# Feature-major chunks in the Mamba-2 layer of a fused attention and state-space kernel

## The chip, the cores and the metric

The kernel runs on one core of one Trainium2 chip. The time is that of one launch on the device, in microseconds, as the median of several runs. Beside it stands one profiled execution, with its trace: start and duration of every instruction on TensorE (PE, with its weight loads PEld), VectorE (DVE), ScalarE (ACT), GpSimd (POOL) and the queue of SyncE (SP), which issues most DMAs.

## The reference

Two layers over 1024 latent tokens and 256 context tokens, width 1024: windowed attention, then a gated bidirectional Mamba-2 (SSD) mixer, which is where the change lies. Cut to that layer:

```
z, xbc, dt_raw = split(h @ w_in)                       # h: adaLN-modulated, normalized
xbc = silu(centred_depthwise_conv(xbc, conv_w, conv_b)) # 5 taps
xs, bm, cm = split(xbc)                                # 8 groups x 4 heads x 64; state 128
dt = softplus(dt_raw + dt_bias)                        # per direction and head
# per direction, in chunks of 128 tokens (a_cs: cumulative sum of dt * A in the chunk)
states = einsum(bm, exp(a_last - a_cs), xs * dt)       # carried from chunk to chunk: h_prev
y_diag = einsum(cm . bm, exp(a_cs_q - a_cs_s), xs * dt)
y_off  = einsum(cm, h_prev, exp(a_cs))
y = y_diag + y_off                                     # of both directions
u = (y_f + y_b + d_skip * xs) * silu(z)
u = u * rsqrt(mean(u * u over a group's 256) + 1e-6)   # per token and group
y_lat = (u * norm_w) @ w_out
h = h + gate * y_lat;  out = rms_normalize(h) * final_norm_w
```

## The kernel before, in words

Activations lie feature-major: 128 features on the partitions, tokens along the free dimension. Big products run in the type fp32r, each as three matmuls: operands are split into a high and a low part (`uH`, `uL` of the layer's input; `wh`, `wl` of a weight tile), and high times high, low times high and high times low are added in PSUM. Smaller products (chunks, states, transposes) run in plain fp32, where one product is two records in the trace (a transpose is one).

The SSD layer (`ssd`) loops over 8 groups, and in each over 8 chunks of 128 latent tokens; group and chunk make a *slot* (`slot`, 64 of them, numbered n). While the slots of group g run, the input projection of group g + 1 (`front`, a generator) is cut into pieces, which `fill(0)` to `fill(4)` deal out inside the slot in the shares of `SEGS`; while the last group's slots run, the output projection (`ssd_out`) takes that place. So PE always has projection matmuls between the slot's small products. The pieces are in model units (`N512`, `N256`, `FRONT`, `OUT`), which only divide the work. Their side work (splitting weights, the convolution's taps, silu) waits in the queue `post` and is taken out at a steady pace. Beside the slots runs the generator `states`, which prepares the next group's context and backward states, a step at each `tick`. The framework then orders the instructions of each engine and of SP's queue by a plan of its own, before the run; on the chip each engine executes its list in that order and waits where an input is late. A wait holds up all that stands behind it on the same engine.

`front` (group g): four x, B and C tiles of 128 features over context and latent tokens (L1143, L1152), then convolution and silu; B and x are also transposed to token-major (`bn`, `xn`). The gate z comes last (L1177): here the token block of `uH`/`uL` is the stationary operand, 128 tokens by 128 of the contraction, and 256 columns of the weight move, so z comes out token-major; tanh and one DVE operation make `sz`.

`slot`, in the order of the code:

- `pcb` = B . C of the chunk (L1282); `po`, the inter-chunk product of C with the forward and the backward state, 256 columns each (L1284, L1285), token-major.
- `M`, the decays of both directions for four heads (`decays`: a predicated copy on DVE, four exponentials on ACT), times `pcb` on DVE (L1286). The rows of cumulative sums for it are loaded by SP two slots ahead (`load_rows`, tiles `fd`, `bd`); POOL adds an offset to `bd` (`offset`).
- the state's step: decay on POOL, product `S` (L1291), addition on DVE.
- `y2` = `po` times exp(a_cs), which lies token-major in `eacs` (L1295).
- `dg`, the diagonal of `pcb`, and `sk`, the skip factor with what the two directions share on the diagonal; POOL multiplies x by `sk`, adds the two halves of `y2`, and adds the former (L1306 to L1308).
- `yd` = M . x, four products of 64 columns (L1311, M stationary); DVE adds it and multiplies by `sz`; ACT squares with a sum, POOL takes the power -0.5, ACT rescales (L1320 to L1329).
- in the next slot, `tail`: two transposes back to feature-major (L1341), each evacuated by ACT with the norm weight (L1342), and a store to DRAM (`uN_d`).

PSUM for these is a ring of three buffers (`psX`): `pcb`, `po`, `S`, `yd` and the tail's tile take them in turn.

`ssd_out` loads the 32 half-rows of features (`feats`, 128 x 512 each), splits them into high and low parts (ACT, DVE) and multiplies by the weights in sweeps (L1571); the last tokens' rows are used at the end of the last sweep.

## Time and profile before

| | us |
|---|---|
| median of 3 runs | 1819.04 (1817.78 to 1820.63) |
| the profiled execution, its own time | 1818.37 |
| its span, first to last instruction | 1816.6 |
| PE busy / DVE / ACT / POOL | 1749.0 / 1166.0 / 869.9 / 811.1 |

The span is what the trace shows; the execution's own time is 1.8 us longer. The attention layer and the norms fill the first 750 us or so, the SSD layer the rest: the first group's projection up to 857 us, the slots from there to 1700, the rest of the output projection and the final norm after that. In the lines of the profile, "x512" is a count, "| busy, mean ns" follow it, and "<-" names what ended the idle time before. In the timeline the first two numbers are start and duration.

### The profile page before, as it was taken

The page shows a single profiled execution, that of the slowest core. Times are in us where ns is not written, and L with a number is a line of the kernel's source. Part 1 is how long each engine was busy: PE and PEld are TensorE (multiplying, and loading weights), DVE is VectorE, ACT ScalarE, POOL GpSimd, SP SyncE. Part 2 cuts the span into 40 slices and gives each one's busy share as a digit, 9 for nine tenths or more (in the row PEclk, how much of TensorE's full clock was granted, in tenths as well). Part 3 has the DMA queues.
Part 4 walks back from the last instruction along what each step waited for, and adds up shares of the span by engine and source line. Part 5 has one row for each costly group of instructions (what it writes and reads, how often), then busy time and mean ns, then how long its engine had stood idle before and what let it go on. Part 6 is the DMA issues. An engine that isn't in the chain of part 4 may idle for free.

```text
span 1816.6 us, 29129 instructions
## 1 busy us (share of the span) xinstructions
PE 1749.0 (96%) x10379; PEld 1500.2 (83%) x10379; DVE 1166.0 (64%) x2125; ACT 869.9 (48%) x1895; POOL 811.1 (45%) x1074
## 2 busy tenths in 40 slices
PE   6999998999999899999999999999999999999997
PEld 3797767788889687778898898989889898988886
DVE  3563536786787766675766748567675857766643
ACT  3521235677788766352444434344353434544522
POOL 2441127554456465303454544646454454644311
PEclk9999999999999999999999999999999999999998
DMA  8768865543345445311322323323332322655542
GB/s 296 285 156 255 261 192 138 119 116 99 99 117 132 118 133 195 112 42 52 86 68 79 93 69 88 82 71 79 78 93 78 82 79 74 188 163 179 163 137 70
DMA packets 209393, 227.89 MB, mean 125 GB/s; under 512 B 16096, under 2 KB 149088, under 8 KB 208224
## 3 DMA queue, kind: packets, MB, share of 16 engines
q1 hardware_dynamic: 175184, 207.38, 38.1%
q0 software_dynamic: 34064, 18.65, 5.6%
q8 instruction: 82, 1.34, 0.3%
q14 instruction: 63, 0.52, 0.1%
HBM read 191.14 MB, written 35.13 MB: 125 GB/s over the span
## 4 chain that ended last, share of the span: by engine, by line
PE 83%; DVE 5%; ACT 4%; DMA 4%; issue 3%; POOL 0%; SPq 0%; DVEq 0%; ACTq 0%; POOLq 0%
PE pj L1152 17%; PE pj L1177 10%; PE pj L1571 7%; PE pj L223 6%; PE pj L225 6%; PE pj L224 6%; PE psD L1143 3%; PE pt L694 3%; PE psX L1311 2%; PE pv L701 2%; PE psD L1236 2%; PE pv L700 2%; PE S L669 2%; PE psX L1285 1%; PE S L670 1%
## 5 line engine op out<-in xcount | busy, mean ns | idle before, releaser
L223 PE MATMUL pj<-uH,wh 128*128 128x256 f32 (+1 forms) x652 | 233.5, 358 | 8.1 <-DVE rope_b L532 2.3
L224 PE MATMUL pj<-uL,wh 128*128 128x256 f32 (+1 forms) x652 | 220.1, 338 | 0.0
L225 PE MATMUL pj<-uH,wl 128*128 128x256 f32 (+1 forms) x652 | 220.1, 338 | 0.0
L211 POOL TENSOR_TENSOR wl<-wr,wh 128x512 fp32r<-128x512 f32 x92 | 121.7, 1326 | 97.4 <-ACT wh L209 96.9
L1152 PE MATMUL pj<-uH,wh 128*128 128x512 f32 x480 | 161.4, 410 | 2.0 <-ACT xn L1088 1.2
L1152 PE MATMUL pj<-uH,wl 128*128 128x512 f32 x480 | 158.5, 403 | 0.0
L1152 PE MATMUL pj<-uL,wh 128*128 128x512 f32 x480 | 157.3, 402 | 0.0
L699 DVE TENSOR_TENSOR pl<-pt,ph 128x512 fp32r<-128x512 f32 x168 | 114.2, 687 | 61.3 <-ACT ph L698 60.4
L223 PEld LDWEIGHTS pj<-uH,wh 128*128 128x128 f32 x652 | 124.7, 191 | 34.9 <-issue 8.6
L1177 PE MATMUL pj<-wh,uH 128*128 128x256 f32 x512 | 148.0, 289 | 3.1 <-ACT xn L1088 3.0
L1177 PE MATMUL pj<-wl,uH 128*128 128x256 f32 x512 | 150.7, 294 | 0.0
L1213 POOL TENSOR_TENSOR xw<-xn,dtdec 128x256 f32<-128x256 f32 x144 | 92.9, 649 | 127.1 <-PE psD L1236 108.5
L1177 PE MATMUL pj<-wh,uL 128*128 128x256 f32 x512 | 149.5, 292 | 0.0
L1342 ACT ACTIVATE uT<-psX,nw 128x128 f32<-128x128 f32 x128 | 46.7, 365 | 193.2 <-PE psX L1341 193.1
L225 PEld LDWEIGHTS pj<-uH,wl 128*128 128x128 f32 x652 | 124.4, 191 | 14.8 <-issue 1.7
L673 DVE CUSTOM_DVE_ANT_0 sm<-S,mask,nsink 128x640 f32<-128x640 f32 (+2 forms) x160 | 118.7, 772 | 26.5 <-PE S L670 14.5
L224 PEld LDWEIGHTS pj<-uL,wh 128*128 128x128 f32 x652 | 124.9, 192 | 11.5 <-issue 2.8
L209 ACT CAST wh<-wr 128x512 fp32r<-128x512 f32 (+1 forms) x132 | 84.8, 645 | 102.5 <-PE pj L224 78.7
L698 ACT CAST ph<-pt 128x512 fp32r<-128x512 f32 x168 | 97.5, 585 | 64.5 <-PE pt L694 58.9
L675 ACT ACTIVATE sm<-sm,nm 128x640 f32<-128x640 f32 (+2 forms) x160 | 118.5, 742 | 12.6 <-DVE nm L673 12.3
L1152 PEld LDWEIGHTS pj<-uL,wh 128*128 128x128 f32 x480 | 90.1, 188 | 19.0
L1152 PEld LDWEIGHTS pj<-uH,wh 128*128 128x128 f32 x480 | 89.1, 188 | 19.6 <-ACT bn L1088 2.0
(383 smaller groups left out, 4999.8 us busy)
## 6 DMA issues: line engine op xcount, KB each, us to landing
fd<-acs SPq DMA_DIRECT2D x64, 256.0 KB, 5.0
bd<-acs SPq DMA_DIRECT2D x64, 256.0 KB, 5.2
wr<-w_x SPq DMA_DIRECT2D x31, 512.0 KB, 3.8
wr<-w_sk SPq DMA_DIRECT2D x24, 512.0 KB, 4.0
wr<-wg SPq DMA_DIRECT2D x44, 256.0 KB, 4.6
qs<-q POOLq DMA_DIRECT2D x40, 256.0 KB, 3.9
wr<-wo SPq DMA_DIRECT2D x40, 256.0 KB, 2.7
wada<-w_ad SPq DMA_DIRECT2D x8, 1024.0 KB, 6.4
```

Of the source, the lines that this page charges most:

```text
L211: (eng or nc.vector).tensor_tensor(l, raw, h, op=ALU.subtract)
L223: self.nc.tensor.matmul(ps, lh, rh, start=first and i == 0, stop=False)
L224: self.nc.tensor.matmul(ps, lh, rl, start=False, stop=False)
L225: self.nc.tensor.matmul(ps, ll, rh, start=False, stop=last and i == n - 1)
L673: nc.vector.tensor_tensor_reduce(out=sm[:, :W], in0=Sv, in1=self.mask[:, m0 : m0 + W], scale=-SCALE, scalar=self.nsink[:, 4 * j + r : 4 * ...
L675: nc.scalar.activation(sm[:, :W], sm[:, :W], AF.Exp, bias=nm[:, r : r + 1], scale=-1.0, accum_out=sums[:, r : r + 1])
L698: nc.scalar.copy(ph, ptf)
L699: nc.vector.tensor_sub(pl, ptf, ph)
L1152: nc.tensor.matmul(raw[:, 512 * i : 512 * i + 512], l[:, k, :], r[i][:, k, :], start=k + y == 0, stop=k == KT - 1 and y == 2)
L1177: nc.tensor.matmul(pj[:, c], l, r[:, k, :], start=c % 2 + q + k + y == 0, stop=c % 2 == 1 and q == 1 and k == 3 and y == 2)
L1213: nc.gpsimd.tensor_tensor(xw, X(st, c).rearrange("p (r h) -> p r h", r=R), self.dtdec[:, c, hd(d, g)].unsqueeze(2).broadcast_to([P, R, HP] ...
L1571: nc.tensor.matmul(banks[x], l[:, z, sl], r, start=k == 2 * qs[0] and y == 0, stop=k == 2 * qs[-1] + 1 and y == 2)
```

## The change

The slot is turned from token-major to feature-major.

- `z` is computed like x: the weight tile is stationary, 512 tokens move; `w_z` is laid out in tiles of 128 features.
- `po` has the states as the stationary operand and C as the moving one: four products of 128 columns. Its factor exp(a_cs) now lies along the free dimension, the same on all partitions of a head: it is stored to DRAM once (`eacs_d`, 16 stores) and loaded by two broadcasting DMAs a slot (`load_scale`, tile `eb`), two slots ahead.
- The skip goes on M's diagonal: DVE makes `dg` and `sk` before `y2`; POOL multiplies the identity by `sk` (into the tile of `eb`, once `y2` has read it) and adds it to M. The product of x with `sk` and its addition to y are gone.
- `yd` has x as the stationary operand, 64 columns a head, and M moves, 128 columns; odd heads write the upper half of the partitions, even heads the lower half.
- y is stored without its norm. ACT squares it, POOL adds the two halves (`sq`), and the tail is one product of `sq` with a column of ones, one small ACT operation, and in every fourth slot a power on POOL over four columns and a store of 512 factors (`rn_d`).
- `ssd_out` loads those factors with a broadcast (`scales`, in the buffers of `bT` and `cT`), POOL multiplies each feature tile by them, ACT applies the norm weight while it makes the high part, DVE makes the low part with the weight in the same operation.
- `SEGS` gives the first stretch of a slot 3.5 of 9.8 shares (1.5 of 9.9 before). At start-up four transposes and four copies go, since `eacs` is not made token-major any more.

The core of the diff, dedented; `ps2` gets three buffers for `yt` and two for `eb`:

```diff
 N512, N256 = 0.229, 0.120
-FRONT = 4 * 48 * N512 + 3 * 24 * N256 + 8 * 24 * N256
+FRONT = 4 * 48 * N512 + 3 * 24 * N256 + 4 * 24 * N512
...
 LATE = 3.0
-SEGS = (1.5, 2.0, 2.0, 2.2, 2.2)
+SEGS = (3.5, 1.8, 1.5, 1.5, 1.5)
...
 self.acs_d = t(dr, [1, 64, LAT], F32, "acs")
+self.eacs_d = t(dr, [2, G, 2, 2, LAT], F32, "eacsd")
...
 nc.scalar.activation(acs, acs, AF.Exp)
+for d in range(2):
+    for f in range(2):
+        for r in range(R):
+            row = 64 * d + 32 * f + r
+            nc.sync.dma_start(self.eacs_d[r % 2, :, d, r // 2, 512 * f : 512 * f + 512], acs[row : row + 29 : 4, :512])
...
         pt = t(ps, [P, 4, 2, 2, 32], F32, "psX")
-        for x, y in enumerate((dd, acs, dt, ln)[: 1 if b == 4 else 4]):
+        for x, y in enumerate((dd, dt, ln)[: 1 if b == 4 else 3]):
...
             nc.scalar.copy(self.dtdec[:, c, :].rearrange("p f (d h) -> p d f h", d=2), pt[:, 0])
-            nc.scalar.copy(self.eacs[:, c, :].rearrange("p f (d h) -> p d f h", d=2), pt[:, 1])
-            nc.scalar.copy(self.dtb[:, c, :], pt[:, 2, 1])
-            nc.scalar.copy(self.vf[:, c, :], pt[:, 3, 0])
-            nc.vector.tensor_sub(self.vo[:, c, :], pt[:, 3, 1], self.vf[:, c, :])
+            nc.scalar.copy(self.dtb[:, c, :], pt[:, 1, 1])
+            nc.scalar.copy(self.vf[:, c, :], pt[:, 2, 0])
+            nc.vector.tensor_sub(self.vo[:, c, :], pt[:, 2, 1], self.vf[:, c, :])
...
 def wz(q):
-    return lambda: weights(a["w_z"][g, q], 4, 256)
+    return lambda: weights(a["w_z"][2 * g + q], KT, P)
...
 for i in range(2):
-    pj = t(ps, [P, 4, 256], F32, "pj2")
+    pj = t(ps, [P, 2, 512], F32, "pj2")
...
         need(ww)
-        for c in range(4):
-            for k in range(4):
-                u, v = uH[i][:, 4 * q + k, c * P : (c + 1) * P], uL[i][:, 4 * q + k, c * P : (c + 1) * P]
-                for y, (l, r) in enumerate(((u, ww["h"]), (u, ww["l"]), (v, ww["h"]))):
-
-                    nc.tensor.matmul(pj[:, c], l, r[:, k, :], start=c % 2 + q + k + y == 0, stop=c % 2 == 1 and q == 1 and k == 3 and y == 2)
-                    yield N256
+        for k in range(KT):
+            for y, (l, u) in enumerate(((ww["h"], uH), (ww["h"], uL), (ww["l"], uH))):
+                nc.tensor.matmul(pj[:, q], l[:, k, :], u[i][:, k, :], start=k + y == 0, stop=k == KT - 1 and y == 2)
+                yield N512
...
             post.extend(st["next"]["steps"])
-    sz = t(self.pz, [P, 4, 256], F32, "sz")
+    sz = t(self.pz, [P, 2, 512], F32, "sz")
...
         nc.vector.scalar_tensor_tensor(sz, in0=sz, scalar=1.0, in1=pj, op0=ALU.add, op1=ALU.mult)
-        st["sz"] += [sz[:, x] for x in range(4)]
+        st["sz"] += [sz[:, :, x * P : (x + 1) * P] for x in range(4)]
...
 self.uN_d = [t(self.dr, [2, P, P * NCH], F32, f"uN{g}") for g in range(G)]
+self.rn_d = [[t(self.dr, [1, 512], F32, f"rn{g}_{i}") for i in range(2)] for g in range(G)]
...
+eb = {}
+
+def load_scale(n):
+    if n < G * NCH:
+        g, c = divmod(n, NCH)
+        x = eb[n] = t(ps2, [P, 2, 2, P], F32, "eb")
+        for f in range(2):
+            src = self.eacs_d[f : f + 1, g, :, :, c * P : (c + 1) * P].rearrange("o d e q -> o (d e) q")
+            nc.sync.dma_start(x[64 * f : 64 * f + 64].rearrange("p d e q -> p (d e) q"), src.broadcast_to([64, R, P]))
+
...
 cs = slice(c * P, (c + 1) * P)
-xc = X(st, c).rearrange("p (r h) -> p r h", r=R)
...
 nc.tensor.matmul(pcb, st["bT"][:, cs], st["cT"][:, cs], start=True, stop=True)
-po = t(ps, [P, 512], F32, "psX")
-nc.tensor.matmul(po[:, :256], st["cT"][:, cs], flat(st["hf"]), start=True, stop=True)
-nc.tensor.matmul(po[:, 256:], st["cT"][:, cs], flat(st["hb"][c]), start=True, stop=True)
+po = t(ps, [P, 2, 2, P], F32, "psX")
+for d, h in enumerate((st["hf"], st["hb"][c])):
+    for e in range(2):
+        nc.tensor.matmul(po[:, d, e], flat(h)[:, e * P : (e + 1) * P], st["cT"][:, cs], start=True, stop=True)
...
     st["hf"] = hn
-y2 = t(ps2, [P, 2, R, HP], F32, "y2")
-nc.vector.tensor_tensor(y2, po.rearrange("p (d r h) -> p d r h", d=2, r=R),
-                        self.eacs[:, c, :].rearrange("p (d q) -> p d q", d=2)[:, :, 4 * g : 4 * g + 4].unsqueeze(3).broadcast_to([P, 2, R, HP]), op=ALU.mult)
+x = eb.pop(n)
+y2 = t(ps2, [P, 2, 2, P], F32, "y2")
+sk = t(ps2, [P, R + 1], F32, "sk")
+dg, sk = sk[:, R:], sk[:, :R]
+nc.vector.tensor_tensor_reduce(out=y2[:, 0, 0], in0=pcb, in1=self.ident, scale=1.0, scalar=0.0, op0=ALU.mult, op1=ALU.add, accum_out=dg)
+nc.vector.scalar_tensor_tensor(sk, in0=self.dtb[:, c, 4 * g : 4 * g + 4], scalar=dg, in1=self.dsk[:, 4 * g : 4 * g + 4], op0=ALU.mult, op1=ALU.add)
+nc.vector.tensor_tensor(y2, po, x, op=ALU.mult)
+xv = x.rearrange("p d e q -> p (d e) q")
+nc.gpsimd.tensor_tensor(xv, self.ident.unsqueeze(1).broadcast_to([P, R, P]), sk.unsqueeze(2).broadcast_to([P, R, P]), op=ALU.mult)
+nc.gpsimd.tensor_tensor(M, M, xv, op=ALU.add)
 fill(0)
-xs = t(ps2, [P, R, HP], F32, "xs")
-dg = t(ps2, [P, 1], F32, "dg")
-nc.vector.tensor_tensor_reduce(out=flat(xs)[:, :P], in0=pcb, in1=self.ident, scale=1.0, scalar=0.0, op0=ALU.mult, op1=ALU.add, accum_out=dg)
-sk = t(ps2, [P, R], F32, "sk")
-nc.vector.scalar_tensor_tensor(sk, in0=self.dtb[:, c, 4 * g : 4 * g + 4], scalar=dg, in1=self.dsk[:, 4 * g : 4 * g + 4], op0=ALU.mult, op1=ALU.add)
-y = ys[n % 2]
-yf = y[:, :256]
-yv = yf.rearrange("p (r h) -> p r h", r=R)
-nc.gpsimd.tensor_tensor(xs, xc, sk.unsqueeze(2).broadcast_to([P, R, HP]), op=ALU.mult)
-nc.gpsimd.tensor_tensor(yv, y2[:, 0], y2[:, 1], op=ALU.add)
-yadd = nc.gpsimd.tensor_tensor(yv, yv, xs, op=ALU.add)
+y = t(ps2, [P, 2, P], F32, "yt")
+yadd = nc.gpsimd.tensor_tensor(y, y2[:, 0], y2[:, 1], op=ALU.add)
+load_scale(n + 2)
...
 for r in range(R):
-    nc.tensor.matmul(yd[:, r * HP : (r + 1) * HP], M[:, r], X(st, c)[:, r * HP : (r + 1) * HP], start=True, stop=True)
+    e, f = divmod(r, 2)
+    nc.tensor.matmul(yd[64 * f : 64 * f + 64, e * P : (e + 1) * P], X(st, c)[:, r * HP : (r + 1) * HP], M[:, r], start=True, stop=True)
...
         offset(n + 1)
-nc.vector.tensor_add(yv, yv, yd[:, :256].rearrange("p (r h) -> p r h", r=R))
-ymul = nc.vector.tensor_mul(yf, yf, st["sz"][c])
-ss = t(ps2, [P, 1], F32, "ss", 2)
-nc.scalar.activation(y2.rearrange("p d r h -> p (d r h)")[:, :257], y[:, :257], AF.Square, scale=1.0 / 16.0, accum_out=ss)
-nc.gpsimd.tensor_tensor(ss, ss, self.half, op=ALU.pow)
+nc.vector.tensor_add(y, y, yd[:, :256].rearrange("p (e q) -> p e q", e=2))
+ymul = nc.vector.tensor_mul(y, y, st["sz"][c])
+nc.sync.dma_start(self.uN_d[g][:, :, cs].rearrange("e p n -> p e n"), y)
+nc.scalar.activation(y2[:, 0], y, AF.Square, scale=1.0 / 16.0)
+sq = t(ps2, [P, P], F32, "sq")
+nc.gpsimd.tensor_tensor(sq, y2[:, 0, 0], y2[:, 0, 1], op=ALU.add)
...
         nM = decays(n + 1)
-nc.scalar.activation(yf, yf, AF.Copy, scale=ss)
...
 def tail(pt):
-    uT = t(ps2, [P, 2, P], F32, "uT")
-    for e in range(2):
-        nc.tensor.transpose(pt[:, e * P : (e + 1) * P], yf[:, e * P : (e + 1) * P], self.ident)
-        nc.scalar.activation(uT[:, e], pt[:, e * P : (e + 1) * P], AF.Copy, scale=self.nw[:, 2 * g + e : 2 * g + e + 1])
-    nc.sync.dma_start(self.uN_d[g][:, :, cs].rearrange("e p n -> p e n"), uT)
+    nc.tensor.matmul(pt[:, :1], sq, self.ones[:, :1], start=True, stop=True)
+    if c % 4 == 0:
+        self.ss = t(ps2, [P, 4], F32, "ss", 2)
+    ss = self.ss
+    nc.scalar.activation(ss[:, c % 4 : c % 4 + 1], pt[:, :1], AF.Identity, bias=self.eps4)
+    if c % 4 == 3:
+        nc.gpsimd.tensor_tensor(ss, ss, self.mhalf, op=ALU.pow)
+        nc.sync.dma_start(self.rn_d[g][c // 4].rearrange("o (c p) -> p (o c)", c=4), ss)
...
 ws, feats, dst, ready, put = [], [], {}, set(), [0]
+scales = [t(sp, [P, LAT], F32, x) for x in ("bT", "cT")]
...
 i, k = order[len(feats)]
+if k % 2 == 0:
+    nc.sync.dma_start(scales[k // 2 % 2][:, k // 4 % 2 * 512 :][:, :512], self.rn_d[k // 2][i].broadcast_to([P, 512]))
...
 hi, lo = dst[order[n]]
+k = order[n][1]
+
+def scale():
+    nc.gpsimd.tensor_tensor(feats[n], feats[n], scales[k // 2 % 2][:, k // 4 % 2 * 512 :][:, :512], op=ALU.mult)
+
+def high():
+    nc.scalar.activation(hi, feats[n], AF.Copy, scale=self.nw[:, k : k + 1])
...
 def low():
-    nc.vector.tensor_sub(lo, feats[n], hi)
+    nc.vector.scalar_tensor_tensor(lo, in0=feats[n], scalar=self.nw[:, k : k + 1], in1=hi, op0=ALU.mult, op1=ALU.subtract)
...
-post.extend([lambda: nc.scalar.copy(hi, feats[n]), low])
+post.extend([scale, high, low])
...
 w = i["ssd_w_in"][0]
-d["w_z"] = np.ascontiguousarray(w[:, :SW].reshape(2, 4, P, G, 256).transpose(3, 0, 2, 1, 4)).reshape(G, 2, P, 1024)
+d["w_z"] = tiles(w[:, :SW])
...
```

16 lines of the change are left out of this document (6 added, 10 removed).

## The prediction

> **What bounds the kernel now.** I read the page's busy table first, then the sums over stretches of time, then the table of waits, and at last the timeline of TensorE (PE), matmul by matmul.
>
> ```profile
> span 1816.6 us, 29129 instructions
> PE 1749.0 (96%) x10379; PEld 1500.2 (83%) x10379; DVE 1166.0 (64%) x2125; ACT 869.9 (48%) x1895; POOL 811.1 (45%) x1074
> ```
>
> The average mixes stages. The change lies in the state-space layer, from some 800 us on, so the stretches of that layer matter: one steady group of eight slots, the last group's slots (which carry the output projection), and the end.
>
> ```profile
> core 0: us, PE busy (x) PEld busy (x) DVE busy (x) ACT busy (x) POOL busy (x), PEclk, DMA share, GB/s
> 1067.00:1173.00 106.00, 105.25 (x653) 94.19 (x653) 72.34 (x124) 45.80 (x106) 53.77 (x75) 1.00 0.29 79
> 1589.00:1700.00 111.00, 110.78 (x553) 92.60 (x552) 70.98 (x120) 51.43 (x113) 49.58 (x60) 1.00 0.59 176
> ```
>
> PE is busy for 105.25 of 106.00 us at full clock, VectorE (DVE) for 68%, POOL for 51%, ScalarE (ACT) for 43%. The largest entry of PE in the table of waits, over seven groups (sum, times, longest), is this:
>
> ```profile
> PEld pj L1177 <- ACT xn L1088: 4.0, 7, 0.6
> ```
>
> So PE's issue sets the time there: a microsecond taken from PE's stream is a microsecond of the kernel, and work moved among the other three costs nothing until PE has to wait for it. "Busy" is not the price of a matmul, since records overlap; the price is the step from one start to the next. All prices for PE below are such steps.
>
> **z with x's layout.** Of the 192 matmuls of 256 columns per group, 96 of 512 columns remain.
>
> ```profile
> L1177 PE MATMUL pj<-wh,uH 128*128 128x256 f32 x512 | 148.0, 289 | 3.1 <-ACT xn L1088 3.0
> 1143.05 0.28 PE L1177 MATMUL pj<-wh,uH 128*128 128x256 f32 x1
> ...
> 1144.49 0.28 PE L1177 MATMUL pj<-wh,uH 128*128 128x256 f32 x1
> 1105.00 0.63 PE L1152 MATMUL pj<-uL,wh 128*128 128x512 f32 x2
> ...
> 1108.22 0.62 PE L1152 MATMUL pj<-uH,wl 128*128 128x512 f32 x2
> ```
>
> The mean of 289 ns would promise far too much. Twelve matmuls start between the first two stamps: 1.44/12 = 0.120 us a step. Fourteen of 512 columns start between the last two: 3.22/14 = 0.230. A group goes from 192 x 0.120 = 23.04 to 96 x 0.230 = 22.08 us; eight groups save 7.7 us. Tanh, product and weight splits keep their element counts.
>
> **The transposes of y.** 64 slots lose two each.
>
> ```profile
> 1103.16 1.00 PE L1311 MATMUL psX<-xn,fd 128*128 128x64 f32 x8
> 1104.00 0.28 PE L1341 MATMUL psX<-ident,y 128*128 128x128 f32 x1
> ...
> 1121.48 0.28 PE L1143 MATMUL psD<-uH,wl 128*128 128x256 f32 x1
> 1121.60 0.27 PE L1341 MATMUL psX<-ident,y 128*128 128x128 f32 x1
> 1121.63 0.36 PE L1143 MATMUL psD<-uH,wh 128*128 128x256 f32 x1
> 1121.83 0.28 PE L1143 MATMUL psD<-uL,wh 128*128 128x256 f32 x1
> ```
>
> From 1121.48 to 1121.83 stand two matmuls of 0.12 and one transpose: 0.35 - 0.24 = 0.11. So 128 x 0.11 = 14.1 us go. The start-up loses four more: 0.4 us.
>
> **The column product that replaces them.** `sq` is the stationary operand, one column of ones moves. An fp32 product is two records, each with its own 128-column weight load, and one moving column hides no load.
>
> ```profile
> 60.22 0.61 PE L418 MATMUL aps<-sel,arow 128*128 128x2 f32 x4
> 60.76 0.64 PE L410 MATMUL aps<-wada,cs 128*32 128x256 f32 x8
> 61.32 0.50 PE L466 MATMUL pj<-uL,wh 128*128 128x512 f32 x1
> 61.66 0.39 PE L467 MATMUL pj<-uH,wl 128*128 128x512 f32 x1
> ```
>
> L418 is the nearest kind: two such products in 0.54 us, 0.27 each with the turn to another shape. The eight records of L1311, whose 64 columns hide no load either, take 0.84, or 0.21 a product. I take 0.24: 64 x 0.24 = 15.4 us come, between 13.4 and 17.3. The transposes are thus paid back on PE; what is freed is ACT.
>
> **yd turned over.** Now: four products, 0.84 us a slot. After: each has 64 weight columns and 128 moving ones, and writes an upper or a lower half of the partitions. A pass of 128 fp32 columns is half of one of 256:
>
> ```profile
> 1122.43 0.59 PE L1284 MATMUL psX<-hf,cT 128*128 128x256 f32 x2
> 1122.86 0.59 PE L1285 MATMUL psX<-hb,cT 128*128 128x256 f32 x2
> ```
>
> Two passes of 256 take 0.43, so one of 128 takes 0.107. Eight passes in a row would be 0.86, no gain; pairs side by side 0.43. That column parts of the array do run side by side shows in L410 above: eight passes of 256, 1.72 us in a row, are through in 0.56, four abreast. They carry a surcharge: 0.56 - 0.43 = 0.13 inside, and 0.34 instead of 0.23 for the next matmul, so 0.24 in all. L942 has the very shape of the new products (64 columns, though alone) and pays no surcharge:
>
> ```profile
> 770.15 0.39 PE L1114 MATMUL pj<-uH,wfh 128*128 128x512 f32 x1
> 770.38 0.39 PE L942 MATMUL psX<-uL,wdth 128*64 128x512 f32 x1
> 770.60 0.39 PE L942 MATMUL psX<-uH,wdtl 128*64 128x512 f32 x1
> 770.83 0.40 PE L1114 MATMUL pj<-uL,wfh 128*128 128x512 f32 x1
> ```
>
> The low end is 0.43 and the high end 0.43 + 2 x 0.24 = 0.91, where the order cuts the block in two. I take 0.60, nearer to L410's 0.67 than to L942's 0.43, since L410 alone shows both overlap and fp32: 64 x 0.24 = 15.4 us saved; from 26.2 saved to 4.5 lost.
>
> The Trainium skill, "TensorEngine Tiling (Array Packing)", Key Properties, says that tiles load weights and multiply in parallel, and that a change of tiling mode drains the array. L410 agrees with both; L942's even 0.23 us steps show no drain. By the parallel rule alone the block would be at its low end, by the drain rule at L410's 0.67.
>
> **The inter-chunk product.** Two products of 256 columns (0.86 us together) become four of 128: eight passes of 0.107, as long as their weight loads (0.105 a record in L1311). No change.
>
> **DVE, ACT, POOL.** DVE keeps its operations, two of them earlier in its order. ACT loses the two scaled evacuations and the rescale, more than a microsecond a slot. POOL's order on the way to yd changes most.
>
> ```profile
> L1265 POOL TENSOR_TENSOR bd<-bd,vo 128x512 f32<-128x512 f32 x64 | 68.4, 1069 | 26.1 <-DMA bd<-acs 26.1
> L211 POOL TENSOR_TENSOR wl<-wr,wh 128x512 fp32r<-128x512 f32 x92 | 121.7, 1326 | 97.4 <-ACT wh L209 96.9
> L1306 POOL TENSOR_TENSOR xs<-xn,sk 128x256 f32<-128x256 f32 x64 | 46.0, 719 | 76.5 <-DVE sk L1302 76.4
> L1308 POOL TENSOR_TENSOR y<-y,xs 128x256 f32<-128x256 f32 x64 | 48.3, 754 | 3.3
> L1324 POOL TENSOR_TENSOR ss<-ss,half 128x1 f32<-128x1 f32 x64 | 37.7, 590 | 105.5 <-ACT y L1323 105.5
> L1295 DVE TENSOR_TENSOR y<-psX,eacs 128x512 f32<-128x512 f32 x64 | 43.9, 686 | 35.4 <-PE psX L1285 34.7
> L1038 DVE SCALAR_TENSOR_TENSOR cacc<-pj,cw,cacc 128x1022 f32<-128x1022 f32 x32 | 40.9, 1277 | 7.9 <-ACT cacc L1034 7.8
> ```
>
> The diagonal times the skip factor costs some 1.07 (512 elements with broadcasts, as L1265), its addition to M 1.33 (two full operands, as L211), the sum of squares about 0.38 (half of L1308). Gone are 0.72, 0.75 and three quarters of 0.59. Net +0.87 a slot: 6.7 becomes 7.6 us of a slot of some 13. That is cover enough in sum, but the first two now stand between the inter-chunk product and yd. After that product ends, DVE multiplies (0.69), POOL works 1.07 + 1.33, and M is ready after 3.1 us, hand-overs between the engines not counted. PE has in between the state product (0.43) and the slot's first stretch of projection: a group's projection is 192 x 0.230 + 72 x 0.120 + 22.1 = 74.9 us, 9.4 a slot, of which 3.5/9.8, or 3.3 us, comes first (1.4 before). That is 3.8 against 3.1: covered, with 0.7 to spare, and not covered where a convolution tap (L1038, 1.28) stands ahead on DVE, unless the order lets more projection go first. Queued behind POOL's wait are the sum of the two halves, bd's offset (which DVE needs for the next M) and the state weights; the slot's remaining six microseconds cover them.
>
> **DMA queues.**
>
> ```profile
> fd<-acs SPq DMA_DIRECT2D x64, 256.0 KB, 5.0
> 802.07 0.42 SPq L1006 DMA_DIRECT2D eald<-et  x1
> 802.58 0.37 SPq L1057 DMA_DIRECT2D wr<-w_z  x1
> 831.12 2.65 PE pj L1177 x20
> ```
>
> The row scales add two loads of 128 KB a slot, asked for two slots (some 26 us) ahead; the same amount in fd lands in 5.0. Each issue holds SP for about 0.4 us: 0.8 more per slot. Sixteen small stores at start-up take SP some 16 x 0.42 = 6.7 us, ahead of the z weights at 802.58; these are first used at 831.12. All hidden. If that cover were gone, they would cost their 6.7 us once.
>
> **Output projection.** Each of 32 features gets a pass on POOL (1.33) before ACT and DVE; 12 matmuls of 0.23 use it up in 2.8, so the rate holds: in the stretch from 1589, POOL's 49.6 us grow by 8 x 0.87 and 14 x 1.33 to 75 of 111. The factors lie in the previous group's `bT` and `cT`, free only after its last slot, and must land first.
>
> ```profile
> 1582.18 0.59 PE L1285 MATMUL psX<-hb,cT 128*128 128x256 f32 x2
> 1594.95 0.58 PE L1571 MATMUL pj<-uH,wh 128*128 128x512 f32 x1
> ```
>
> The last use is near 1582.6; with 5.0 for the landing, 1.33 on POOL and about 1.3 for high and low part, the first feature is ready near 1590.3, before 1594.95. I charge 3 us for this entry and for new small waits in the slots, between 0 and the first rival's price. The last group's factors are used at the end of the last sweep, which is 16 x 12 x 0.23 = 44 us long.
>
> **Sum.** -7.7 - 14.1 - 0.4 + 15.4 - 15.4 + 3 = -19.2: a span of 1797.4 us. The profiled execution took 1818.37, 1.8 above its span; the median of the three runs, 1819.04, is 0.7 above it. So 1797.4 + 2.5 = 1800.
>
> **Rivals.**
>
> *POOL takes the place* (slower). M's addition comes late and yd waits at the head of PE, with the whole projection behind it. If a 1.28 us tap stands ahead on DVE in each slot, 0.58 of it is left after the 0.7 to spare: 0.58 x 64 = 37 us, a time of 1837. It decides from 0.31 us a slot (20/64). For it: a spare time shorter than one tap. Against it: PE's longest wait now is 0.6 us, none of the long ones is for POOL, and other projection can go ahead of yd.
>
> *The halves buy nothing.* Surcharges at both edges, or a block cut by another matmul, keep yd at 0.76 to 0.91: 10 to 20 us are missing, a time of 1810 to 1820. For it: L410's edges. Against it: L942.
>
> The drain rule of the Trainium skill's tiling page speaks for this rival; here it would be paid twice a slot.
>
> *The halves overlap fully*, at L942's edges: yd at 0.43 saves 11 us more: 1789.
>
> **Chances.** The forecast (1794 to 1806) 0.45, full overlap 0.20, halves for nothing 0.18, POOL 0.17. The range 1785 to 1823 leaves out the far part of POOL's case and the best corner of full overlap. A measurement of this kernel tells about 0.2% (3.6 us) from no change: faster 0.76 (forecast, overlap, most of the third case), same 0.07, slower 0.17.
>
> **What would show it.** z's matmuls at steps of 0.23, 768 of them; pairs of yd starting within hundredths of a microsecond of each other and the block's length between 0.43 and 0.91; the column product at 0.21 to 0.27; a steady group of some 103 us instead of 105.5; POOL near 60%; waits of PE for POOL's M near nothing. Wrong it is if PE waits for M by more than 0.3 us a slot, or falls below 97% in the groups for another reason.

## The result, and the profile after

The changed kernel takes 2013.85 us (median of four runs, 2012.61 to 2025.48) where the kernel before took 1819.05: a ratio of 1.1085, interval 1.1043 to 1.1126, or 195 us slower. Predicted were 1800.

First the busy table of the page of after, the same lines as were shown of before.

```profile
span 2011.9 us, 28315 instructions
PE 1806.8 (90%) x9863; PEld 1480.6 (74%) x9863; DVE 1168.5 (58%) x2123; ACT 820.2 (41%) x1699; POOL 901.5 (45%) x1122
```

No engine is fuller than before in its share; PE went from 96% to 90%. So time went into waits, and into a slower clock: PE stands for 205 us of its span instead of 68, and it is busy for 58 us more than before although it has less to do. The mean granted clock of the span is 0.946 where it was 0.990, so some 109 us of full clock were withheld instead of 18. Sums over stretches of after (columns: stretch, its length, busy time of PE, weight loads, DVE, ACT, POOL, granted clock, DMA share, GB/s):

```profile
1067.00:1173.00 106.00, 93.97 (x499) 76.99 (x498) 60.17 (x108) 34.14 (x72) 53.63 (x71) 0.90 0.40 89
1239.00:1364.00 125.00, 113.12 (x589) 92.94 (x589) 70.00 (x124) 39.23 (x83) 58.62 (x76) 0.92 0.37 86
1330.00:1334.50 4.50, 1.65 (x7) 0.73 (x5) 0.87 (x2) 0.37 (x1) 4.17 (x6) 1.00 0.16 21
1334.50:1345.00 10.50, 7.91 (x30) 5.72 (x30) 4.83 (x12) 1.96 (x6) 8.64 (x13) 0.67 0.35 89
```

In the stretch quoted of before PE was busy for 105.25 of 106 us at full clock; now 93.97, at 0.90. A steady group lasts some 124 us and not 105.5. The second line is one group, nearly to the slice: 0.08 x 125 = 10 us of its 19 too many are clock, by its 0.92. The third and fourth lines lie inside that group: PE stands, POOL is full (4.17 of 4.50), and then the granted clock is 0.67.

From group to group (first `pcb` to first `pcb`; the end of the span for the last), the loss is 33 us in the first group (137.1 for 103.9), 115 in the six that follow (747.2 for 632.6) and 50 in the last with all that comes after it (272.6 for 222.7).

The timeline of PE in one group of after: its first `pcb`, the last product of z, the last 512-column product of the projection with the state products behind it (`psD` <- `xw`, `bn`), and the next group's first `pcb`.

```profile
1239.16 0.47 PE L1293 MATMUL psX<-cT,bT 128*128 128x128 f32 x2
...
1316.13 0.39 PE L1178 MATMUL pj<-uH,wl 128*128 128x512 f32 x1
...
1330.32 0.63 PE L1156 MATMUL pj<-uH,wl 128*128 128x512 f32 x2
1331.00 0.70 PE L1238 MATMUL psD<-xw,bn 128*128 128x256 f32 x2
1334.82 0.70 PE L1238 MATMUL psD<-xw,bn 128*128 128x256 f32 x2 [3.13 <-POOL xw L1215]
1336.04 1.12 PE L1323 MATMUL psX<-fd,xn 128*64 128x128 f32 x8 [0.52 <-POOL fd L1315]
...
1363.99 0.47 PE L1293 MATMUL psX<-cT,bT 128*128 128x128 f32 x2
```

z, the last part of the projection, is through 48 us before the group ends. In the kernel before it ended with the group:

```profile
1383.10 0.28 PE L1177 MATMUL pj<-wh,uL 128*128 128x256 f32 x1
1383.21 0.38 PE L1282 MATMUL psX<-cT,bT 128*128 128x128 f32 x2
```

So the order issues the projection early, five slots of 16 to 18 us consume it, and the last three slots (from 1324.1, 1337.5 and 1349.4) have little left to put into their waits: from 1331 on only 24 products for the context tokens, at 1357.6. The table of waits of after, 843 to 1800 us, shows which waits (sum, times, longest; `xw` is the weighted x, `hb` the backward state that DVE adds up, `fd` is M):

```profile
PEld psD L1238 <- DVE hb L1250: 41.3, 14, 3.5
PEld psD L1238 <- POOL xw L1215: 31.9, 17, 3.5
PEld psX L1323 <- POOL fd L1315: 14.8, 16, 3.2
```

Only 14.8 us are waits of `yd` for M itself. The larger ones are the next group's state products behind it, whose inputs POOL and DVE make in between. The long chain is paid for where the cover has run out, under other names.

DVE's timeline of a covered slot of after (M times `pcb`, then `sk`, then `y2`):

```profile
1277.39 0.68 DVE L1298 TENSOR_TENSOR fd<-fd,psX 128x512 f32<-128x512 f32 x1
...
1280.52 0.22 DVE L1311 SCALAR_TENSOR_TENSOR sk<-dtb,sk,dsk 128x4 f32<-128x4 f32 x1
1280.65 0.68 DVE L1312 TENSOR_TENSOR y<-psX,eb 128x512 f32<-128x512 f32 x1
```

and POOL's behind it:

```profile
1281.41 1.04 POOL L1314 TENSOR_TENSOR eb<-ident,sk 128x512 f32<-128x512 f32 x1 [4.32 <-DVE y L1312]
1282.41 0.74 POOL L1318 TENSOR_TENSOR yt<-y 128x256 f32<-128x256 f32 x1
1283.11 1.04 POOL L1277 TENSOR_TENSOR bd<-bd,vo 128x512 f32<-128x512 f32 x1
1284.11 1.29 POOL L1315 TENSOR_TENSOR fd<-fd,eb 128x512 f32<-128x512 f32 x1
```

Before, M was ready when DVE had multiplied it by `pcb` (0.68). Now 8.0 us pass from the start of that to the end of the addition (1277.39 to 1285.40): a convolution tap and a weight split on DVE ahead of `sk` (1.28 and 1.22), the diagonal's buffer held by `y2`, then the spreading, and 1.7 us of other POOL work ahead of the addition. The median over the 64 slots is 8.0 us too.

### The profile page after: what moved, and what is told of

The parts are those of the page before. It is cut to its first block, busy times and chain, and to the rows that moved or that the text cites. A ratio compares the mean times of both kernels' runs of the same rounds, so it can differ in the third digit from the quotient of the medians.

```text
span 2011.9 us, 28315 instructions
## 1 busy us (share of the span) xinstructions
PE 1806.8 (90%) x9863; PEld 1480.6 (74%) x9863; DVE 1168.5 (58%) x2123; ACT 820.2 (41%) x1699; POOL 901.5 (45%) x1122
## 3 DMA queue, kind: packets, MB, share of 16 engines
q8 instruction: 78, 1.28, 0.3%
## 5 line engine op out<-in xcount | busy, mean ns | idle before, releaser
L1215 POOL TENSOR_TENSOR xw<-xn,dtdec 128x256 f32<-128x256 f32 x144 | 88.7, 616 | 234.2 <-PE psX L1303 145.6
L1156 PE MATMUL pj<-uH,wh 128*128 128x512 f32 x480 | 151.6, 397 | 6.8 <-ACT bn L1092 6.8
L1156 PE MATMUL pj<-uH,wl 128*128 128x512 f32 x480 | 152.8, 397 | 0.9 <-DVE wl L1069 0.9
L1332 DVE TENSOR_TENSOR yt<-yt,psX 128x256 f32<-128x256 f32 x64 | 26.9, 420 | 203.9 <-PE psX L1323 125.4
L225 PEld LDWEIGHTS pj<-uH,wl 128*128 128x128 f32 x652 | 124.1, 191 | 14.8 <-issue 1.7
L224 PEld LDWEIGHTS pj<-uL,wh 128*128 128x128 f32 x652 | 124.8, 191 | 11.5 <-issue 2.8
L673 DVE CUSTOM_DVE_ANT_0 sm<-S,mask,nsink 128x640 f32<-128x640 f32 (+2 forms) x160 | 118.8, 772 | 23.6 <-PE S L670 11.7
L1238 PE MATMUL psD<-xw,bn 128*128 128x256 f32 x176 | 71.6, 496 | 64.2 <-DVE hb L1250 41.4
L675 ACT ACTIVATE sm<-sm,nm 128x640 f32<-128x640 f32 (+2 forms) x160 | 118.5, 742 | 11.7 <-DVE nm L673 11.4
L1592 PE MATMUL pj<-uH,wh 128*128 128x512 f32 x192 | 79.3, 417 | 39.3 <-ACT uH L1544 35.6
L1314 POOL TENSOR_TENSOR eb<-ident,sk 128x512 f32<-128x512 f32 x64 | 69.6, 1087 | 99.0 <-DVE y L1312 99.0
L1156 PEld LDWEIGHTS pj<-uH,wl 128*128 128x128 f32 x480 | 90.7, 189 | 19.9 <-DVE wl L1069 1.3
```

Of the source, the lines that this page charges most:

```text
L224: self.nc.tensor.matmul(ps, lh, rl, start=False, stop=False)
L225: self.nc.tensor.matmul(ps, ll, rh, start=False, stop=last and i == n - 1)
L673: nc.vector.tensor_tensor_reduce(out=sm[:, :W], in0=Sv, in1=self.mask[:, m0 : m0 + W], scale=-SCALE, scalar=self.nsink[:, 4 * j + r : 4 * ...
L675: nc.scalar.activation(sm[:, :W], sm[:, :W], AF.Exp, bias=nm[:, r : r + 1], scale=-1.0, accum_out=sums[:, r : r + 1])
L1156: nc.tensor.matmul(raw[:, 512 * i : 512 * i + 512], l[:, k, :], r[i][:, k, :], start=k + y == 0, stop=k == KT - 1 and y == 2)
L1215: nc.gpsimd.tensor_tensor(xw, X(st, c).rearrange("p (r h) -> p r h", r=R), self.dtdec[:, c, hd(d, g)].unsqueeze(2).broadcast_to([P, R, HP] ...
```

## The experiments

The theory from these tables: the skip's way over POOL into M makes the slot's chain longer than its cover. Rivals: the new shares, the row-scale loads, POOL's pass in the output projection, z. Differences below are against the kernel before as run on the same chip (1815.5 to 1821.2); those without an interval come from single runs. Four runs of e3 lie 9 us apart, so a few microseconds between two single runs say little. The diffs are shortened.

**e1, no skip.** The two POOL lines of the diagonal are gone, so the skip and the diagonal term are left out of the output.

```diff
-nc.gpsimd.tensor_tensor(xv, ident, sk, op=ALU.mult)
-nc.gpsimd.tensor_tensor(M, M, xv, op=ALU.add)
```

> The changed kernel without its two POOL passes over M (the spreading of sk onto a diagonal, L1314, and the addition into M, L1315); the skip and the diagonal term are so left out of the output. Theory: these two passes lie in a chain that each slot has to go through before its yd products (product with pcb, diagonal, sk, spread, addition), and behind POOL's other work; the chain sets the slot. Without them M is ready some 6 us sooner in a slot that has cover (1278.8 for 1285.4) and 3 us sooner in one without, a group comes back from 124 us to 104 to 108, and the whole time is 1800 to 1860 us. Rival, the new shares of the fill: 2000 or more, since the order of the fill stays. Rival, the broadcast loads of the row scales: 1990 or more, as the loads stay. Rival, POOL's scaling in the output projection: 1970 or more, as only the last stage would matter and that stays.

Measured: 1866.3 us, 45 over before; 150 of the 195 us are gone. The rivals that leave these lines alone can't have caused that part by themselves.

**e2, skip on DVE**, in the place of the two POOL lines.

```diff
+for r in range(R):
+    nc.vector.scalar_tensor_tensor(M[:, r], in0=ident, scalar=sk[:, r:r+1], in1=M[:, r], op0=ALU.mult, op1=ALU.add)
```

> The changed kernel with the diagonal added to M by four instructions on DVE (identity times sk plus M, 128x128 each) in the place of the two POOL passes; everything is computed. Theory (a chain through POOL): four passes of about 0.2 to 0.3 us on the engine that has just made sk put M ready at about 1 us behind sk, where POOL took 4.9 us (1280.5 to 1285.4); a group of 106 to 112 us and 1820 to 1890 us in all. Rival, that any engine is as bad since DVE is then the late one: 1950 or more. The rivals of the shares and of the loads: 2000 or more.

Measured: 1883.4, 62 over before. Four passes on the engine that made `sk` put M ready 4.5 us after its start, though they cost 115 us of DVE in all. In DVE's timeline:

```profile
1432.83 0.67 DVE L1298 TENSOR_TENSOR fd<-fd,psX 128x512 f32<-128x512 f32 x1
...
1434.03 0.21 DVE L1311 SCALAR_TENSOR_TENSOR sk<-dtb,sk,dsk 128x4 f32<-128x4 f32 x1
1434.16 0.68 DVE L1312 TENSOR_TENSOR y<-psX,eb 128x512 f32<-128x512 f32 x1
1435.15 2.23 DVE L1315 SCALAR_TENSOR_TENSOR fd<-ident,sk,fd 128x128 f32<-128x128 f32 x4
```

A steady group is full again at full clock (stretch of one group of e2):

```profile
1405.40:1511.90 106.50, 105.43 (x587) 86.42 (x586) 82.94 (x156) 38.91 (x81) 43.00 (x60) 1.00 0.50 100
```

DVE at 78% does no harm; it was where the work stood in the chain that did. The row-scale loads are still there, so they cost nothing in these groups.

**e4, the shares of before.**

```diff
-SEGS = (3.5, 1.8, 1.5, 1.5, 1.5)
+SEGS = (1.5, 2.0, 2.0, 2.2, 2.2)
```

> The changed kernel with the shares of the fill as they were before (1.5, 2.0, 2.0, 2.2, 2.2 for 3.5, 1.8, 1.5, 1.5, 1.5). Theory (a chain through POOL): the chain stays as long and only the place of the projection's products within a slot moves; 1990 to 2060 us. Rival, that the shares put the projection in the wrong places: the time comes back by most of the loss, to 1800 to 1880 us.

Measured: 2024.8. The shares are out.

**e5, projection paced.** Each projection product is ordered behind the last `yd` written ahead of it.

```diff
+with self.tc.issue_after(self.pace):
     cost = next(work, None)
```

> The changed kernel with every projection product ordered behind the last yd product that was written ahead of it in the program, so that the order can't fill a slot's wait with the projection products of later slots; the work is the same. Theory: the order fills a chain of 17 us in the first five slots of a group with the whole group's projection and then has none for the last three. With its own share only, a slot has 11 us of PE work and waits for its chain every time; if a chain without foreign work is 12 to 14 us, as in the last slots of a group now, the time is 1850 to 1960 us. If the chain is 15 us or more whatever the order is, 2010 to 2150 us, and pulling ahead did no harm.

Measured: 2085.6. Every slot then waits for its chain; pulling ahead helped. The chain is too long however the cover is dealt out.

**e9, addition first on POOL.**

```diff
+with self.tc.issue_after(madd.ins):
     yadd = nc.gpsimd.tensor_tensor(y, y2[:, 0], y2[:, 1], op=ALU.add)
```

> The changed kernel with both passes left on POOL, but the sum of the two inter-chunk halves (yadd, L1318), and with it bd's offset (L1277), put behind the addition into M. In the changed kernel POOL does those two, 0.74 and 1.04 us, and in slots with states two or three of 0.62 more, between the spreading and the addition. Theory A (what costs is the place in POOL's order): M is ready 1.8 to 3.1 us sooner in each slot; the sum of the halves comes 1.3 us later, which nobody waits for; 1880 to 1930 us. Theory B (what costs is the length of the two passes themselves with three changes of engine): at most a third of the 131 us that the move to DVE brought comes back; 1970 to 2000 us.

Measured: 1947.4, 127 over before. Between the two theories: the place in POOL's list is worth 68 us, about half of what DVE brought. The chain says the same: from the start of the product with `pcb`, M is ready after 6.1 us (median of the 64 slots), where it was 8.0 in after and 4.6 in e2. That the passes and their changes of engine are the other half is what is left over, not shown by a run.

**e16, the skip alone, in the kernel before.** Identity times `sk` (into the buffer of `y2`) is added to M by POOL; the two operations on x and y go.

```diff
-nc.gpsimd.tensor_tensor(xs, xc, sk, op=ALU.mult)
-yadd = nc.gpsimd.tensor_tensor(yv, yv, xs, op=ALU.add)
+nc.gpsimd.tensor_tensor(xv, ident, sk, op=ALU.mult)
+nc.gpsimd.tensor_tensor(M, M, xv, op=ALU.add)
```

> The kernel before with one part of the change alone: the skip and the shared diagonal go onto M through POOL (identity times sk into the buffer of y2 after the two halves are added, then the addition into M), the product of x with sk and its addition to y go. z, yd, po and the output projection stay as before; everything is computed. Theory, that this chain is the main cause by itself: it brings 60 to 150 us alone: 1880 to 1970. Rival, that it costs so much only together with the turned slot (the shares, the row scales, the column product): less than 30 us, 1815 to 1850.

Measured: 1977.8, 161 over before, the most expensive part by itself. POOL's timeline has the same picture:

```profile
1381.66 0.74 POOL L1305 TENSOR_TENSOR y<-y 128x256 f32<-128x256 f32 x1 [4.29 <-DVE y L1299]
1382.36 1.04 POOL L1265 TENSOR_TENSOR bd<-bd,vo 128x512 f32<-128x512 f32 x1
1383.36 2.02 POOL L1307 TENSOR_TENSOR y<-ident,sk 128x512 f32<-128x512 f32 x1
1385.34 0.61 POOL L1213 TENSOR_TENSOR xw<-xn,dtdec 128x256 f32<-128x256 f32 x1
1385.91 1.29 POOL L1308 TENSOR_TENSOR fd<-fd,y 128x512 f32<-128x512 f32 x1
```

And z is again through 48 us before its group ends (last product 1313.51, next `pcb` 1361.35). The main cause is shown from both sides.

**e8, products of one half in a row** (on e2).

```diff
-for r in range(R):
+for r in (0, 2, 1, 3):
```

> The version with the skip on DVE (e2_skip_dve, 1883.4 us), with the four yd products of a slot in the order 0, 2, 1, 3, so that products of the same column half follow each other and only the middle pair lies in different halves. If halves run side by side, as the prediction's 0.60 us a block takes it, the block grows from 0.67 by 0.2 to about 0.87 us: 64 x 0.2 = 13 us, 1893 to 1898 us. If side by side buys nothing (the rival), the block stays at its length and the time at 1881 to 1886.

Measured: 1898.8, 16 more than e2 against before. The size is the one expected, but by luck: whole blocks still take 0.60, and their products still start in pairs, 13 ns apart, so the new order doesn't keep the halves from running side by side. Other products cut more of the blocks in two, and the steps of `yd` sum to 6.97 us a group for 5.96. So 8 us are `yd`; the rest is order.

**e3, e14, e17, e15: z.** z alone in the kernel before; the same in products of 256 columns; the same paced as in e5; and the old z in e2. In e3, e14 and e17 the gate meets y in another layout, so the output is not the reference's; the same holds for e15. The diff is in words.

```diff
-192 x matmul(pj[:, c], uH-block, w[256 columns])
+96 x matmul(pj[:, q], w-tile, uH[512 columns])          # e3
+96 x 2 x matmul(pj[:, q, half], w-tile, uH[256 columns]) # e14
```

> The kernel before with one part of the change alone: z is computed like x, with weights as the stationary operand and 512 columns moving, 96 matmuls a group for 192 of 256 columns. y is still computed with tokens on partitions, so the gate meets it in the wrong layout and the values of the output are not the reference's; the work is the same. The prediction's term: 96 x 0.230 for 192 x 0.120 us a group, eight groups: 7.7 us less, 1811 us, a ratio of 0.996. If the steps of 512 columns or the gate's strided read in DVE bring a new wait: 1819 or more.

Measured: a ratio of 1.0154 (1.0126 to 1.0183), 28 us slower. A miss, and the largest surprise.

> The kernel before with z alone computed like x (e3_z_only, 1846.6 us), but each of its products cut into two of 256 columns with the same weights, so that PE has 192 steps of 0.12 us a group as before. If the coarse steps (0.23 us, fewer places at which the slot's products can go in between) cost the 28 us: 1815 to 1828. If the new order of the whole group does, whatever the step: 1835 to 1860. If z's layout or its gate in DVE does: 1847 to 1858, as the PE part is 8 us longer.

Measured: 1818.1, 1.5 over before. Layout, gate and weights are those of e3, and they cost nothing. (The model's price of a group, `FRONT`, is that of before here and the new one in e3.) With the halves the order is that of before: z ends at the group's end again.

```profile
1382.26 0.40 PE L1175 MATMUL pj<-uH,wl 128*128 128x256 f32 x2
1382.50 0.38 PE L1280 MATMUL psX<-cT,bT 128*128 128x128 f32 x2
```

In e3 it ends 9.2 us earlier, and products of the x tile of the group after follow it:

```profile
1394.59 0.39 PE L1174 MATMUL pj<-uH,wl 128*128 128x512 f32 x1
1394.82 0.62 PE L1152 MATMUL pj<-uH,wh 128*128 128x512 f32 x2
...
1403.81 0.39 PE L1279 MATMUL psX<-cT,bT 128*128 128x128 f32 x2
```

> The kernel before with z alone computed like x (e3_z_only, 1846.6 us), with every projection product ordered behind the last yd product written ahead of it, as in e5_paced, so that the order can't issue a slot's projection in an earlier slot (gate and output as in e3_z_only). In e3_z_only z is through 9 us before the group's end (1394.6 of 1403.8), in the kernel before at its end (1383.1 of 1383.2). Theory: the 28 us are cover spent early; the slot's chain without the new skip is 8 to 10 us and fits under an even share, so z keeps what its steps save: 1808 to 1822. If pacing costs as it did in the changed kernel (72 us more), the chain is long here too: 1860 to 1920. If z's 512-column form itself is at fault: 1840 to 1855.

Measured: 1.0235 (1.0218 to 1.0252). Slower still, so an even spread isn't the cure that I expected. PE's timeline at the group's border shows why: the states of the next group form a chain of their own, and nothing was left to put between its products.

```profile
1294.49 0.70 PE L1233 MATMUL psD<-xw,bn 128*128 128x256 f32 x2 [1.59 <-DVE hb L1245]
1296.11 1.22 PE L1233 MATMUL psD<-xw,bn 128*128 128x256 f32 x2 [0.92 <-DVE hb L1245]
1297.91 1.22 PE L1233 MATMUL psD<-xw,bn 128*128 128x256 f32 x2 [0.58 <-DVE hb L1245]
```

> The version with the skip on DVE (e2_skip_dve, 1883.4 us) with z computed as before, 192 matmuls of 256 columns a group; the gate so meets y in the wrong layout and the output's values are not the reference's, the work is the same. z alone brought 28 us to the kernel before. If z costs this much wherever it stands: 1850 to 1860. If the 28 us came from the order of the one kernel, the PE term alone counts, and the old z costs 8 to 10 us: 1888 to 1900.

Measured: 1888.9, 10 more than e2 against before. In sum that is about the new z's term, but not by stage: with the old z the first group is 11.7 us shorter (105.4 for 117.1) and the seven behind it are between 1.6 shorter and 4.4 longer, and the two spans differ by 5.4. So this doesn't show that the new z saves its term. What z costs or saves hangs on the order it brings. Whether the grain of its products or the model's price of them changes that order wasn't told apart.

**e13 and e18, the new shares alone, in the kernel before.** The edit is e4's, the other way.

> The kernel before with nothing changed but the shares of the fill (3.5, 1.8, 1.5, 1.5, 1.5 for 1.5, 2.0, 2.0, 2.2, 2.2). No instruction comes or goes; only the order changes. If the time before hangs on its order, so that any new order costs some 20 to 40 us: 1835 to 1860. If the order counts for little as long as the work is the same: 1815 to 1825, and the 28 us of z have a cause in z.

> The kernel before with the new shares of the fill alone, once more and timed against it in rounds; one look gave 1812.1 beside 1816.6 us, and a group of 103.4 to 104.8 us for 105.5. If the order with a longer first stretch is better: a ratio of 0.996 to 0.998. If that look was chance: 0.999 to 1.001.

Measured: 1812.1 in a single run, then a ratio of 0.9957 (0.9944 to 0.9970), 7.8 us faster. A changed order doesn't cost 28 us as such. This version beats both kernels.

**e6, e7, e10, e11: the last group**, where e2 still loses 36 us (258.7 for 222.7); 13 more go in its first group (117.1 for 103.9), which no run here explains. All four are on e2: without POOL's pass over the features; with the pass on DVE; with factors that are always ready; with factors loaded later.

```diff
-post.extend([scale, high, low])
+post.extend([high, low])                       # e6
-nc.gpsimd.tensor_tensor(feats[n], feats[n], scales, op=ALU.mult)
+nc.vector.tensor_tensor(feats[n], feats[n], scales, op=ALU.mult)  # e7
-nc.sync.dma_start(scales, self.rn_d[k // 2][i])
+nc.sync.dma_start(scales, self.rn_d[0][0])     # e10; e11 moves the line from fetch to split
```

> The version with the skip on DVE, without POOL's pass over the features of the output projection (L1541); the normalization by tokens is so left out, the loads of its factors stay. The last group with what follows takes 258.7 us there and took 222.7 before the change. Theory: POOL's pass is what makes the features late (ACT waits 64.9 us for it in that stage; a pass takes 1.2 to 1.9 us beside the state work of the same engine); 25 to 36 us go: 1847 to 1858 us. Rival, the store and load of the factors holds the features' loads in the queue: the time stays above 1870.

> The version with the skip on DVE, with POOL's pass over the features moved to DVE (128x512, about 0.7 us each); everything is computed. If POOL's pass is slow and queued behind the states, 10 to 30 us come back: 1853 to 1873 us. If what counts is that one more engine stands in the chain and that the factors arrive late (the first one waits until the previous group's last use of the buffer), 1875 to 1885 us.

> The version with the skip on DVE (1883.4 us), with every load of the token factors in the output projection reading the first group's factors, which were stored long before; the normalization so has wrong factors, and nothing else changes. In that version SP's queue stands 16.5 us at these loads until the factors' store has landed (some 8 us each), with the loads of the projection's weights behind it. Theory (the queue's wait): 15 to 30 us go, 1853 to 1868 us. Rival (POOL's pass after all, or the slot's longer way in the last group): 1878 or more.

> The version with the skip on DVE, with the load of a group's factors issued not with the loads of its features, four or more features ahead, but when the first of these features is to be scaled; everything is computed. Theory (the queue's wait): the store has mostly landed by then, so the queue stands less; but the scaling waits for the load itself, 2 to 5 us each; 1860 to 1880 us. Rival: no change, 1880 to 1887.

Measured against before, where e2 has +62: +58, +72, +67 and +64. None brings the stage back. In e6 the last group is 15.7 us shorter, but the one before it is 12.0 longer (123.0 for 111.0). ACT's waits for the pass (52.6 us from 1600 to 1800 in e2) become, without it, waits of the same ACT for the features' loads (52.9). What PE waits for in e2 in that stretch is spread out:

```profile
PE pj L1592 <- ACT uH L1544: 9.7, 2, 8.3
PE psX L1297 <- DVE yt L1332: 6.4, 1, 6.4
PE psD L1238 <- DVE hb L1250: 3.8, 2, 2.2
```

The 36 us stay open; shown is only that neither POOL's pass nor the factors' store is the one cause.

**e12, no column product** (on e2).

```diff
-nc.tensor.matmul(pt[:, :1], sq, self.ones[:, :1], start=True, stop=True)
-nc.scalar.activation(ss[:, c % 4], pt[:, :1], AF.Identity, bias=self.eps4)
+nc.scalar.activation(ss[:, c % 4], sq[:, :1], AF.Identity, bias=self.eps4)
```

> The version with the skip on DVE without the column product of sq with ones (L1351); the sum over partitions is so left out, and ACT reads one column of sq for it. The prediction gave the product 0.24 us a slot; the trace of this version shows 0.33 where it stands between projection matmuls. By the trace 64 x 0.33 = 21 us go, 1862 us; by the prediction's price 15 us, 1868 us; by more than that, 1855 or less, if the wait of the product for ACT and POOL in PE's queue counts too.

Measured: 1921.6, 106 over before: 44 more, with less work. The order moved (a group of 112 us, waits of PE for `hb` of 14.7 us where e2 has 4.6), so this says nothing on the product's price. It does suggest that the order an edit brings can cost tens of microseconds by itself; the 133 to 161 us of the skip are far above that.

## Why the prediction was wrong, point by point

**The step that failed** is the one on DVE, ACT and POOL: "That is cover enough in sum", "3.8 against 3.1: covered, with 0.7 to spare", and with it the 3 us charged for new waits. The 3.1 us were durations alone, counted from the end of the inter-chunk product. From there M is ready after 9.3 us in after (median of the 64 slots, 4.8 at least), and after 8.0 from the start of its product with `pcb`: the durations, a tap and a weight split on DVE ahead of `sk`, and 1.7 us of POOL work that the order put between the two passes (2.8 in a slot that carries states, the one at 1331). I had "queued behind POOL's wait" the other way round: the sum of the halves, the offset and the state weights went ahead of the addition. The POOL rival had the mechanism and the sign, at 0.17; its price of 0.58 us a slot was far too small, since POOL's skip is worth 133 (against e2) to 161 us (e16), 2.1 to 2.5 a slot. Its limit, a tap of 1.28 ahead on DVE, left POOL's own list out.

"Other projection can go ahead of yd" was right, and no comfort: what goes ahead in one slot is missing in another. The prediction looked at one slot's cover and never at the group's: 75 us of projection for eight slots of 12 to 18. Nor did its sum have a term for the clock, which fell behind the waits (0.92 in the group above).

**PE's terms.** `yd` in halves: right where a block is whole. In after all 64 are, and at full clock they take 0.59 from their start to the next product (0.60 predicted); the pairs start 7 ns apart. "Overlap fully" falls. "Halves buy nothing" falls in after; in e2, where other products cut blocks in two, it mostly came true: 5.96 us a steady group for 6.42 before by the steps (6.90 for 7.69 with what the product behind each block starts late), where 1.93 were to be saved. At the price of after they would take 37.8 us, for 51.9 before, 14 saved; with the clock down and products waiting in some slots they sum to 43.6, so 8.3 were saved of 15.4. The column product: two records in 0.24 to 0.25, as predicted; the pair `pcb` behind it takes 0.30 where it took 0.22. z: 0.23 a step and 96 steps a group, right (22.38 us, with waits, for 22.08); no run shows the saving itself: z alone cost the kernel before 28 us, and the 10 us between e15 and e2 don't lie where the term puts them. The inter-chunk product, "no change", is nearly right: with what the product behind each block starts late, it takes 7.25 us a group in e2 for 6.91 before, 0.04 a slot.

**The group of 103 us.** With the skip on DVE it is 106.5 at a full PE, so PE's small terms were some 3 us a group too hopeful. In the group quoted of e2 five of eight `yd` blocks are cut in two by other products; cut, one takes 0.36 + 0.58 us (at 1447.84 and 1448.84) for 0.59. The range of the prediction had that (0.91), its sum did not.

**The output projection.** The entry was charged with 3 us; in e2 PE waits 8.3 there for the first feature, and the stage loses 36 in all.

**The DMA queues** hide what was said to be hidden in the steady groups: e1 and e2 run full with all new loads in place.

**The signs** given for being wrong: PE under 97% in the groups came true at once (89% of the stretch from 1067). The other, waits for M above 0.3 us a slot, hardly did: 14.8 us are 0.26 a slot. It was the wrong place to look, since the waits moved to the state products.

## What to carry to other kernels

When an edit puts an operation of another engine between two matmuls, count the chain from its first input to its last output through that engine's list, with all that the order may put in between; durations alone gave 3.1 us where 9.3 passed. Cover is a stock of the whole loop: work pulled ahead to fill one wait leaves a hole later, and the wait shows there under another name, so look at when the filler work ends, not only at who waits. Run each part of a compound change alone: here one part cost 161 us, one 28 or nothing by the order that came with it, and the part that seemed mere bookkeeping, the shares, was the only one of the three to gain.

## What the runs showed of the hardware

Short gaps of PE cost twice here. In e17, with the three gaps shown above (3.1 us together), the granted clock falls to half, from the second of them at 1295.6 until 1305.9, as the sums over stretches show:

```profile
1296.00:1304.00 8.00, 7.31 (x20) 5.71 (x21) 1.31 (x4) 0.00 (x0) 3.86 (x7) 0.50 0.19 65
1304.00:1308.00 4.00, 4.00 (x20) 3.38 (x19) 0.69 (x1) 0.00 (x0) 0.10 (x1) 0.77 0.15 36
```

The 512-column products step at 0.427 us there and at 0.230 from 1306.0 on, although PE has no gap behind 1297.9. The Trainium skill, "TensorE: Matmul & The Clock Gate", Part 1, knows a half and a full clock, with a return after about 3.4 us of sustained work. The two levels agree; the return took some 8 us here (from 1297.9 to 1305.9).

POOL slows beside DVE. The state weights (L1215, 128x256) take 0.61 us in most slots of e2 and 1.59 in twelve places, of which the second line is one:

```profile
1338.20 0.61 POOL L1215 TENSOR_TENSOR xw<-xn,dtdec 128x256 f32<-128x256 f32 x1 [2.44 <-PE psX L1303]
...
1646.80 1.59 POOL L1215 TENSOR_TENSOR xw<-xn,dtdec 128x256 f32<-128x256 f32 x1
```

At 1646.80 DVE was making a weight's low part from two operands in memory (1645.94, 1.98 us, where the split at 1429.46 took 1.21). All twelve stand beside such a split, for 1.12 to 1.13 us; at 1338.20 DVE was busy too, but with one of its two operands in PSUM (`psX`). The Trainium skill, "GPSIMD Engine Reference", section 8, says that POOL shares its memory interfaces with VectorE and contends with instructions that have two inputs there; this row agrees. POOL's durations from a quiet stage are a lower bound where DVE splits weights.
